# Layer 0's output projection in fixed steps on TensorE, with layer 1's first weights, K and Q beside and ahead of its last tile

## The chip, the cores and the metric

The kernel runs on one core of a Trainium2 chip. The metric is the device time of one execution in microseconds, lower is better, given as the median of three runs. A difference is read against the spread of such runs.

## The reference

A backbone of two post-norm layers over 1024 latent tokens and 256 context tokens of width 1024. Layer 0 is multi-head latent attention with 16 heads, layer 1 differential attention with 8 heads; both gate their output before the output projection. Cut to what the change touches:

```python
for i in range(DEPTH):                       # DEPTH = 2
    shift, scale, gate = adaln(c, ada_w[i], ada_b[i])
    h = x * (1.0 + scale) + shift            # the same for the context, with its own vectors
    o, o_c = mixer_i(h, h_c)                 # o is already multiplied by silu(its gate)
    x = layer_norm(ALPHA * x + gate * (o @ out_w[i]), ln_g[i], ln_b[i])
    if i < DEPTH - 1:
        ctx = layer_norm(ALPHA * ctx + gate_c * (o_c @ out_w[i]), ln_g[i], ln_b[i])

# layer 1, diff_mixer: the projections of h come first
q, k, v, gate = split(h @ w_in, 4)           # rotary on q and k, then two softmaxes a head
lam_full = exp(sum(lam[0] * lam[1])) - exp(sum(lam[2] * lam[3])) + lambda_init
```

## The kernel before

Tokens are taken in ten tiles of 128 rows: 0 to 7 are latent tokens, 8 and 9 the context. Matrix products that need the precision are made of three matmuls each, with both operands split into a high and a low part (`mm3`, lines 185 to 187; `split`, lines 176 and 177; `split16`, lines 181 and 182, which also scales).

**Layer 0's last head.** While its last step is retired, the context tiles are multiplied by their gate, turned (`turn_out`, line 833: four transposes for a half, then a split on ScalarE and VectorE, then the other half) and multiplied by the output weights (`mm_out`). This part has a written TensorE order.

**Layer 0's output.** Then comes a loop over the tiles in the order 8, 9, 0 to 7, with no written order: a planner puts the instructions of every engine, TensorE and the DMA queues too, in an order by when they can start in its own model of time. For a latent tile:

- `out_y` loads o (line 903) and its gate g (904), multiplies them on GpSimd (905), turns the product in banks "c" (833) and makes two halves y of 512 columns, in banks "a" and "b", 24 matmuls each.
- `out_z` makes z from y: times the gate row (922), plus the residual (923, loaded at 942), statistics (924, 926), 1/std on GpSimd (`rstd_of`, lines 159 and 160), and the normalisation in place (928).
- z times the norm's gain (958, VectorE) plus its bias (959, GpSimd) is written to memory for layer 1's residual (960).
- z is turned in banks "d" (965). Scale and shift, which fold the norm's gain and bias and layer 1's modulation, make h: a product on VectorE (967) and a sum on GpSimd (969), for each half. ScalarE casts h to its high part h1H (972), GpSimd makes the low part h1L (973).

The two context tiles begin at the z step, since their y is there already.

**Layer 1's start.** Behind the loop stands `prod_w(0, 0)`, the weights of Q and K of head 0: loads of two halves, squares summed on ScalarE (1026), a small matmul against ones (1029), a power-of-two scale in small steps on VectorE and GpSimd, and a split (1048). It is followed by lambda (1058 to 1072) and by a written TensorE order: K in chunks of 512, 512 and 256 tokens (`prod_k1`), Q in two chunks (`prod_q1`), with `prod_w(0, 1)`, the weights of V and the gate, woven in, then V and the gate (`prod_v1`). Attention follows in steps of one head and one tile (scores at lines 1191 and 1192); beside each step runs a part of the next head's projections, and in the last head layer 1's output.

Buffers are allotted by name from pools in order of first use, and a new pool lies over the memory of the closed one before it; a tile waits for those that lie under it.

Of the kernel before, what the change touches and what calls it, by code (L numbers as in the profile page):

```python
# [17 lines left out]
P = 128  # L18
# [35 lines left out]
def hybrid_kernel(  # L54
# [775 lines left out]
    def turn_out(o, hH_, hL_, tb, hh):  # L830

        for j in range(4):
            pe.transpose(tb[:, j * P:(j + 1) * P], o[:, (hh * 4 + j) * P:(hh * 4 + j + 1) * P], idn)
        f = lambda x: x[:, hh * 4:hh * 4 + 4, :].rearrange("p a b -> p (a b)")
        split(f(hH_), f(hL_), tb)
# [6 lines left out]
    for h in range(H0):  # L842
# [8 lines left out]
        if last:  # L851
# [16 lines left out]
            with tc.manual_schedule(engines={ENG[c] for c in MAN}):  # L868
                for t in (8, 9):
                    tb = pair()  # L870
                    for hh in range(2):
                        turn_out(octx[t][0], *tctx[t], tb[:, hh * 512:hh * 512 + 512], hh)
# [25 lines left out]
    def out_y(t, tp):  # L898

        ts = slice(t * P, (t + 1) * P)  # L900
        o = tp.tile([P, D], F32, tag="o", bufs=2, name=nm("o"))
        g = tp.tile([P, D], F32, tag="g", bufs=1, name=nm("g"))
        sp.dma_start(o, o_d[0][ts, :])
        sp.dma_start(g, sg_d[0][ts, :])
        pool.tensor_tensor(o, o, g, op=ALU.mult)
        tH = tp.tile([P, KT, P], F32R, tag="tH", bufs=2, name=nm("tH"))
        tL = tp.tile([P, KT, P], F32R, tag="tL", bufs=2, name=nm("tL"))
        for hh in range(2):
            turn_out(o, tH, tL, bank("c"), hh)
        for hh in range(2):  # L910
            y = bank("ab"[hh])
            mm_out(y, tH, tL, slice(hh * 512, hh * 512 + 512))
            yield y

    def out_z(ys, gate, res_fn, t, tp):

        z = tp.tile([P, D], F32, tag="z", bufs=2, name=nm("z"))
        res, rmul = res_fn(t)
        bs = tp.tile([P, 2, 6], F32, tag="bs", bufs=2, name=nm("bs"))
        for hh, y in enumerate(ys):  # L920
            c = slice(hh * 512, hh * 512 + 512)
            dve.tensor_tensor(z[:, c], y, gate[:, c], op=ALU.mult)
            dve.scalar_tensor_tensor(z[:, c], res[:, c], rmul, z[:, c], op0=ALU.mult, op1=ALU.add)
            dve.bn_stats(bs[:, hh, :], z[:, c])
        mv = tp.tile([P, 4], F32, tag="mv", bufs=2, name=nm("mv"))
        dve.bn_aggr(mv[:, 0:2], bs)
        rstd_of(mv[:, 2:3], mv[:, 1:2], 1.0, 1)
        dve.tensor_scalar(z, z, mv[:, 0:1], mv[:, 2:3], op0=ALU.subtract, op1=ALU.mult)
        return z

    with ow_ctx, spool("o0") as op0:
        gate = [op0.tile([P, D], F32, tag=f"gate0{s}", bufs=1, name=f"gate0{s}") for s in range(2)]
        for s in (1, 0):
            bcast_row(gate[s], gates_d[0, s:s + 1, :])
        gb = []

        zres = {}

        def res0(t):
            r = op0.tile([P, D], F32, tag="res", bufs=2, name=nm("res"))  # L940
            src = xr[t * P:(t + 1) * P, :] if t < 8 else ctxr[(t - 8) * P:(t - 7) * P, :]
            sp.dma_start(r, src)
            zres[t] = r
            return r, ALPHA

        zctx = {t: out_z([yctx[t][:, :512], yctx[t][:, 512:]], gate[1], res0, t, op0) for t in (8, 9)}
        set_banks(a=2, b=2, c=2, d=2)
        for t in (8, 9, 0, 1, 2, 3, 4, 5, 6, 7):
            if t == 0:
                for j, (src, tag) in enumerate(((ln_g, "gate01"), (ln_b, "gb1"))):  # L950
                    gb.append(op0.tile([P, D], F32, tag=tag, bufs=1, name=nm("gb")))
                    bcast_row(gb[j], src[0:1, :])
                    pool.tensor_scalar(gb[j], gb[j], ALPHA, None, op0=ALU.mult)
            s = 0 if t < 8 else 1
            z = out_z(out_y(t, op0), gate[0], res0, t, op0) if t < 8 else zctx[t]
            if t < 8:
                zr = zres[t]
                dve.tensor_tensor(zr, z, gb[0], op=ALU.mult)
                pool.tensor_tensor(zr, zr, gb[1], op=ALU.add)
                sp.dma_start(zn_d[t * P:(t + 1) * P, :], zr)  # L960
            hb = op0.tile([P, KT, P], F32, tag="hb", bufs=1, name=nm("hb"))
            for hh in range(2):
                tb = bank("d")
                for j in range(4):
                    pe.transpose(tb[:, j * P:(j + 1) * P], z[:, (hh * 4 + j) * P:(hh * 4 + j + 1) * P], idn)
                ks = slice(hh * 4, hh * 4 + 4)
                dve.tensor_tensor(hb[:, ks, :], tb.rearrange("p (a b) -> p a b", a=4),
                                  ab1[:, 0, ks, s:s + 1].to_broadcast([P, 4, P]), op=ALU.mult)
                pool.tensor_tensor(hb[:, ks, :], hb[:, ks, :],
                                   ab1[:, 1, ks, s:s + 1].to_broadcast([P, 4, P]), op=ALU.add)  # L970
            ts = slice(t * P, (t + 1) * P)
            act.copy(h1H[:, :, ts], hb)
            pool.tensor_tensor(h1L[:, :, ts], hb, h1H[:, :, ts], op=ALU.subtract)


    a1 = ctx.enter_context(ExitStack())
    wl = a1.enter_context(spool("a1"))
    TAG1 = {"p0": ([P, NTOK], F32, 2), "p1": ([P, NTOK], F32, 1), "ph": ([P, NT, P], F16, 2),
            "pl": ([P, NT, P], F16, 2), "KS0": ([P, NTOK], F16, 2), "KS1": ([P, NTOK], F16, 2),
            "QS0": ([P, SEQ], F16, 2), "QS1": ([P, SEQ], F16, 2), "Q10": ([P, SEQ], F16, 2),  # L980
            "Q11": ([P, SEQ], F16, 2), "vh": ([P, NT, P], F16, 2), "vl": ([P, NT, P], F16, 2),
            "o1": ([P, P], F32, 3), "o2": ([P, P], F32, 2), "mx": ([P, 8], F32, 2), "sm": ([P, 8], F32, 4),
            "ss": ([P, 2], F32, 2), "us": ([P, 1], F32, 3), "es": ([P, 1], F32, 3), "p2s": ([P, 2], F32, 2)}

    TAGP = {"ws": ([P, 4, 256], F32, 3), "wL": ([P, 4, 256], F16, 4), "wH": ([P, 4, 256], F16, 4),
# [9 lines left out]
    for k_, v_ in TAG1.items():  # L995
        rot(wl, v_[0], v_[1], k_, v_[2], first=True)
# [54 lines left out]
    for _ in prod_w(0, 0, lambda: bank("c"), act):  # L1051
        pass
# [476 lines left out]
```

## Time and profile before

| | us |
|---|---|
| runs shown | 1871.88, 1866.82, 1869.04 |
| median | 1869.04 |
| the profiled execution's own time | 1864.35 |
| its span, first to last instruction | 1862.5 |
| mean granted TensorE clock | 0.972 |

The span is the traced part of one execution; 1.85 us of that execution's time lie around it. Where rows of the profile are quoted, a row of a timeline gives start and length in us, engine, line, operation, output and inputs, their shapes and a count; a bracket gives the engine's idle time ahead of it and what ended it. A row of a table by stage gives its two ends and its length, the busy time and number of instructions of each engine, the granted clock, the share of the DMA engines and what they moved. A group's row has busy us, mean ns, and the idle time ahead.

### The profile page before, as it was taken

To read this page: it belongs to the slowest core of one execution; us is meant where nothing else is said; L and a number is where in the kernel's file an instruction comes from. 1 tells how busy PE (TensorE), PEld (TensorE's weight loads), DVE (VectorE), ACT (ScalarE), POOL (GpSimd) and SP (SyncE) were. 2 spreads that over 40 slices of the span, in tenths; PEclk is the share of its full clock that TensorE was granted. 3 is DMA by queue.
4 is the path that set the end of the run, shared out by engine and by line. 5 is a ranking of instruction groups with operands and counts; after the bars stand their busy time and mean duration, and the time that the engine had idled before them with its cause. 6 is when DMAs were issued, how large, how long until landed. Compare 5 with 4: busy or idle time off the path is not lost. (4 is left out here: it accounts for less than half of the span.)

```text
span 1862.5 us, 36549 instructions
## 1 busy us (share of the span) xinstructions
PE 1691.8 (91%) x14468; PEld 1235.3 (66%) x14468; DVE 1242.1 (67%) x2074; ACT 1077.1 (58%) x2143; POOL 831.5 (45%) x739
## 2 busy tenths in 40 slices
PE   7889989999999998869879899999999999988998
PEld 3888965656666565557757575767676666666776
DVE  7445765565565657435764777777877787878674
ACT  3432157877777788801123666676767676767542
POOL 1443026867767676827652313132222222423544
PEclk9999999999999999989989999999999999999999
DMA  8246630111111113134333222222211212214341
GB/s 306 64 132 181 189 107 17 39 40 30 40 44 33 44 40 101 59 130 130 122 129 104 71 62 61 60 63 62 66 52 41 50 50 50 75 42 139 100 132 68
DMA packets 111225, 154.84 MB, mean 83 GB/s; under 512 B 13415, under 2 KB 84679, under 8 KB 111054
## 3 DMA queue, kind: packets, MB, share of 16 engines
q1 hardware_dynamic: 104238, 146.22, 26.4%
q10 hardware_dynamic: 6816, 6.29, 1.0%
q8 instruction: 114, 1.87, 0.4%
q14 instruction: 57, 0.47, 0.1%
HBM read 98.65 MB, written 27.07 MB: 68 GB/s over the span
## 5 line engine op out<-in xcount | busy, mean ns | idle before, releaser
L715 POOL TENSOR_TENSOR pl<-p,ph 128x1024 f16<-128x1024 f32 (+1 forms) x176 | 364.8, 2078 | 147.4 <-ACT ph L714 119.5
L1214 ACT ACTIVATE p<-ps_b,mx 128x512 f32<-128x512 f32 (+1 forms) x384 | 230.6, 618 | 82.7 <-DVE mx L1210 82.5
L695 DVE TENSOR_REDUCE mx<-ps_a 128x1 f32<-128x1024 f32 x128 | 155.5, 1223 | 133.5 <-PE ps_a L693 133.5
L713 ACT ACTIVATE p<-ps_a,esc 128x1024 f32<-128x1024 f32 (+1 forms) x176 | 189.2, 1075 | 94.5 <-PE ps_a L771 88.0
L714 ACT CAST ph<-p 128x1024 f16<-128x1024 f32 (+1 forms) x176 | 177.1, 1006 | 5.5
L1208 DVE TENSOR_REDUCE mx<-ps_b 128x1 f32<-128x512 f32 x256 | 165.5, 681 | 0.0
L784 PE MATMUL ps_d<-Vh,pl 128*128 128x65 f16 x1344 | 145.9, 194 | 3.9 <-POOL pl L715 3.9
L781 PE MATMUL ps_d<-Vh,ph 128*128 128x65 f16 x1344 | 148.0, 195 | 0.0
L783 PE MATMUL ps_d<-Vl,ph 128*128 128x64 f16 x1344 | 146.8, 193 | 0.0
L185 PE MATMUL ps_b<-h1H,wH 128*128 128x512 f16 (+1 forms) x384 | 134.0, 349 | 13.9 <-DVE pl L182 6.8
L185 PE MATMUL ps_b<-wH,h1H 128*128 128x256 f16 x512 | 139.5, 272 | 4.7 <-ACT p L1214 4.5
L187 PE MATMUL ps_b<-wH,h1L 128*128 128x256 f16 x512 | 139.5, 273 | 0.0
L186 PE MATMUL ps_b<-wL,h1H 128*128 128x256 f16 x512 | 139.5, 273 | 0.0
L1191 PE MATMUL ps_b<-KS,QS 128*128 128x512 f16 (+1 forms) x384 | 126.5, 346 | 12.1 <-DVE pl L182 6.1
L1239 POOL TENSOR_TENSOR sm<-sm,us 128x1 f32<-128x1 f32 x64 | 16.2, 253 | 271.5 <-DVE sm L1218 267.5
L781 PEld LDWEIGHTS <-ph 128*128 128x128 f16 x1344 | 123.2, 97 | 18.3 <-issue 5.1
L187 PE MATMUL ps_b<-h1H,wL 128*128 128x512 f16 (+1 forms) x384 | 133.9, 349 | 0.8 <-DVE wL L182 0.8
L186 PE MATMUL ps_b<-h1L,wH 128*128 128x512 f16 (+1 forms) x384 | 133.9, 349 | 0.0
L783 PEld LDWEIGHTS <-ph 128*128 128x128 f16 x1344 | 123.9, 98 | 12.0
L1192 PE MATMUL ps_b<-KS,Q 128*128 128x512 f16 (+1 forms) x384 | 129.3, 345 | 0.0
L769 PE MATMUL ps_a<-qH,KH 100*128 100x512 f16 x320 | 122.0, 381 | 7.7 <-ACT p L713 3.9
L182 DVE SCALAR_TENSOR_TENSOR pl<-ps_b,lcf,ph 128x512 f16<-128x512 f32 (+1 forms) x192 | 117.4, 654 | 16.0 <-ACT ph L181 15.8
(392 smaller groups left out, 5154.7 us busy)
## 6 DMA issues: line engine op xcount, KB each, us to landing
ws<-in_dw SPq DMA_DIRECT2D x30, 512.0 KB, 3.9
adw<-in_ada_w SPq DMA_DIRECT2D x24, 512.0 KB, 4.7
adaw<-in_ada_w SPq DMA_DIRECT2D x16, 512.0 KB, 6.9
g<-sg_d SPq DMA_DIRECT2D x16, 512.0 KB, 3.8
sg_d<-gg ACTq DMA_DIRECT2D x40, 128.0 KB, 3.5
o_d<-op SPq DMA_DIRECT2D x7, 640.0 KB, 3.7
xt<-in_xT SPq DMA_DIRECT2D x16, 256.0 KB, 3.8
wgs<-in_w_in SPq DMA_DIRECT2D x32, 128.0 KB, 2.9
```

Of the source, the lines that this page charges most:

```text
L185: pe.matmul(ps, aH, bH, start=start, stop=False, skip_group_check=skip)
L186: pe.matmul(ps, aH, bL, start=False, stop=False, skip_group_check=skip)
L187: pe.matmul(ps, aL, bH, start=False, stop=stop, skip_group_check=skip)
L695: dve.tensor_reduce(mx[:, t, 0:1], ps, axis=AX.X, op=ALU.max)
L713: act.activation(p32[:, :n], st, AF.Exp, scale=esc0)
L714: act.copy(ph[:, :n], p32[:, :n])
L715: pool.tensor_tensor(pl[:, :n], p32[:, :n], ph[:, :n], op=ALU.subtract)
L781: pe.matmul(pv[:, t, :], ph[:, ts], Vh[:, k, h, :], start=(k == kcs[0] and t == 0), stop=False, skip_group_check=True)
L783: pe.matmul(pv[:, t, :V0], ph[:, ts], Vl[:, k, h, :], start=False, stop=False, skip_group_check=True)
L784: pe.matmul(pv[:, t, :], pl[:, ts], Vh[:, k, h, :], start=False, stop=(k == NT - 1), skip_group_check=True)
L1208: dve.tensor_reduce(mx[:, 2 + 2 * m + i:3 + 2 * m + i], b, axis=AX.X, op=ALU.max, negate=True)
L1214: act.activation(p[m][:, c0:c0 + n], b, AF.Exp, bias=nb, accum_out=sm[:, 2 + 3 * m + i:3 + 3 * m + i])
```

## The change

It has five parts.

1. `turn_out` makes all eight transposes, in two banks, and then both splits.
2. Layer 0's output loop is written in small steps with a fixed TensorE order. For tile t: half 0 of y(t), the turn of z(t-1), the turn of o(t+1), half 1 of y(t). Ahead of the loop stand the turn of o(0) and of z(8); z(9) is turned in tile 0. The loads of o and its gate for tiles 0 and 1 are written ahead of the context's z steps, the norm's rows later, in tile 0.
3. h's scale and shift are made by ScalarE, eight instructions of 128 columns that read the banks and take scale and shift as columns; the product on VectorE and the sum on GpSimd go.
4. Both weight preparations of head 0, `prod_w(0, 0)` and `prod_w(0, 1)`, are made in steps beside tiles 0 to 6, with their loads on ScalarE's queue, and lambda ahead of the loop.
5. Behind tile 7 and ahead of its z turn, TensorE makes K of head 0 for tokens 0 to 511; after that turn K of the context and Q for tokens 0 to 511. `prod_q1` and `prod_k1` take these as made and go on with the rest.

For this the weights of layer 1 lie in a pool of their own below layer 0's output, with high and low part in one tile; layer 1's output, at the end of the kernel, uses the same tiles again for o and its turns.

The core of the diff ("..." where lines are left out):

```diff
-    def turn_out(o, hH_, hL_, tb, hh):
-
-        for j in range(4):
-            pe.transpose(tb[:, j * P:(j + 1) * P], o[:, (hh * 4 + j) * P:(hh * 4 + j + 1) * P], idn)
-        f = lambda x: x[:, hh * 4:hh * 4 + 4, :].rearrange("p a b -> p (a b)")
-        split(f(hH_), f(hL_), tb)
+    def turn_out(o, hH_, hL_, tb):
+
+        for hh in range(2):
+            for j in range(4):
+                pe.transpose(tb[hh][:, j * P:(j + 1) * P], o[:, (hh * 4 + j) * P:(hh * 4 + j + 1) * P], idn)
+        for hh in range(2):
+            f = lambda x: x[:, hh * 4:hh * 4 + 4, :].rearrange("p a b -> p (a b)")
+            split(f(hH_), f(hL_), tb[hh])
...
-            for hh in range(2):
-                tb = bank("d")
-                for j in range(4):
-                    pe.transpose(tb[:, j * P:(j + 1) * P], z[:, (hh * 4 + j) * P:(hh * 4 + j + 1) * P], idn)
-                ks = slice(hh * 4, hh * 4 + 4)
-                dve.tensor_tensor(hb[:, ks, :], tb.rearrange("p (a b) -> p a b", a=4),
-                                  ab1[:, 0, ks, s:s + 1].to_broadcast([P, 4, P]), op=ALU.mult)
-                pool.tensor_tensor(hb[:, ks, :], hb[:, ks, :],
-                                   ab1[:, 1, ks, s:s + 1].to_broadcast([P, 4, P]), op=ALU.add)
...
-    for _ in prod_w(0, 0, lambda: bank("c"), act):
-        pass
-    set_banks(b=8)
...
+        def z_turn(t, tg="d", mid=None):
+            tb = [bank(tg), bank(tg)]
+            for hh in range(2):
+                for j in range(4):
+                    pe.transpose(tb[hh][:, j * P:(j + 1) * P], zs[t][:, (hh * 4 + j) * P:(hh * 4 + j + 1) * P], idn)
+            hb, s, ts = ot("hb", 1, [P, KT, P]), int(t > 7), rows_of(t)
+            for k in range(KT):
+                act.activation(hb[:, k, :], tb[k // 4][:, k % 4 * P:(k % 4 + 1) * P], AF.Identity,
+                               bias=ab1[:, 1, k, s:s + 1], scale=ab1[:, 0, k, s:s + 1])
+            act.copy(h1H[:, :, ts], hb)
+            pool.tensor_tensor(h1L[:, :, ts], hb, h1H[:, :, ts], op=ALU.subtract)
+
+        load_gate(1)
+        load_res(8)
+        load_o(0)
+        load_gate(0)
+        load_res(9)
+        load_o(1)
+        for t in (8, 9):
+            for hh in range(2):
+                z_half(t, hh, yctx[t][:, halves[hh]])
+            z_norm(t)
+        set_banks(a=2, b=2, c=2, d=2)
+        lambda_of()
+        pw = [prod_w(0, i, lambda: bank("c"), act) for i in range(2)]
+        wjobs = {t: [pw[i] for i in js] for t, js in enumerate(((0,), (0,), (0,), (0, 0, 1), (1,), (1,), (1, 1)))}
+        man.enter_context(tc.manual_schedule(engines={ENG["P"]}))
+        turns(0)
+        y1 = bank("b")
+        z_turn(8)
+        for t in range(8):
+            y0 = bank("a")
+            mm_out(y0, *tHL[t], halves[0])
+            z_half(t, 0, y0) if t else load_res(0)
+            for j in wjobs.get(t, ()):
+                next(j)
+            if t == 0:
+                z_half(0, 0, y0)
+                for j, (src, tag) in enumerate(((ln_g, "gate01"), (ln_b, "gb1"))):
+                    gb.append(ot(tag, 1))
+                    bcast_row(gb[j], src[0:1, :])
+                    pool.tensor_scalar(gb[j], gb[j], ALPHA, None, op0=ALU.mult)
+            z_turn(t - 1 if t else 9)
+            if t < 7:
+                turns(t + 1)
+            y1 = y1 if t == 0 else bank("b")
+            mm_out(y1, *tHL[t], halves[1])
+            z_half(t, 1, y1)
+            z_norm(t)
+            z_keep(t)
+            if t < 7:
+                load_res(t + 1)
+            if t < 6:
+                load_o(t + 2)
+        set_banks(b=8)
+        kcols, qcols = slice(P, 2 * P), slice(0, P)
+        made = {0: [*proj1(512, 0, kcols)][-1]}
+        z_turn(7, "b")
+        made[SEQ] = [*proj1(CTX, SEQ, kcols)][-1]
+        made["q"] = [*proj1(512, 0, qcols)][-1]
+        man.close()
...
-        for _ in chain(weave(chain(prod_k1(0), prod_q1(0, 0), prod_q1(0, 1)), prod_w(0, 1), WAT[0]),
+        for _ in prod_q1(0, 0, made.pop("q")):
+            pass
+        later.pop()()
+        for _ in chain(prod_k1(0, made), prod_q1(0, 1),
                        weave(prod_v1(0), prod_w(1, 0), WAT[1])):
```

The steps `load_res`, `load_o`, `turns`, `z_half` (lines 922 to 924 of before, for one half), `z_norm` (926, `rstd_of`, 928) and `z_keep` (958 to 960) hold the same instructions as `out_y` and `out_z` did.

More of the change, by code (lines that the diff above doesn't have):

```diff
@@ L915, in out_z @@
[L915 to L929, printed above, removed]
@@ L1004, in w1 @@
+    wpa = ctx.enter_context(spool("a1w"))
+    for k_, v_ in TAG1.items():
+        rot(wpa, v_[0], v_[1], k_, v_[2], first=True)
+    place = {k_: wpa for k_ in TAG1}
     def w1(tag):
@@ new lines, in hybrid_kernel @@
+    prj = ExitStack()
+    wp = prj.enter_context(spool("a1proj"))
+    for k_, v_ in TAGP.items():
+        rot(wp, v_[0], v_[1], k_, v_[2], first=True)
+    place.update({**{k_: wl for k_ in TAGL}, **{k_: wp for k_ in TAGP}})
+    TAG1.update({**TAGL, **TAGP})
+    wo4 = a1.enter_context(spool("a1ow", side="right"))
+    oHL = [[wo4.tile([P, D], F32R, name=f"oH1{k}"), wo4.tile([P, D], F32R, name=f"oL1{k}")] for k in range(NOW)]
+    gate1 = wo4.tile([P, D], F32, name="gate1")
+    cosB, sinB = w1("cosB"), w1("sinB")
```

216 lines of the change are left out of this document (101 added, 115 removed).

## The prediction

> **What bounds the kernel now.** I read the page's busy shares first, then the stretch that the change touches as a table by stage, then TensorE's timeline in it, and last the engines that TensorE waits for there.
>
> ```profile
> span 1862.5 us, 36549 instructions
> PE 1691.8 (91%) x14468; PEld 1235.3 (66%) x14468; DVE 1242.1 (67%) x2074; ACT 1077.1 (58%) x2143; POOL 831.5 (45%) x739
> ```
>
> TensorE is the bound almost everywhere, so what can be won lies where it waits or runs slow. Busy time by stage (length, then PE, PEld, DVE, ACT, POOL, granted clock, DMA share, GB/s): from the last matmul of the context rows to the end of tile 0, tiles 1 to 7, from there to layer 1's projections, and the rest of these up to the first scores.
>
> ```profile
> 822.00:854.60 32.60, 17.96 (x73) 14.19 (x73) 14.46 (x23) 3.26 (x4) 22.69 (x15) 0.74 0.47 162
> 854.60:959.50 104.90, 95.05 (x449) 75.08 (x447) 75.32 (x91) 14.45 (x21) 67.87 (x47) 0.98 0.35 119
> 959.50:974.00 14.50, 3.28 (x13) 2.32 (x14) 9.44 (x16) 6.46 (x9) 9.55 (x10) 0.64 0.57 204
> 974.00:1022.50 48.50, 48.50 (x340) 33.48 (x341) 20.61 (x49) 15.93 (x37) 11.81 (x13) 0.97 0.40 112
> ```
>
> In the first and third stretch TensorE is busy for 17.96 of 32.60 us and 3.28 of 14.50, at a clock of 0.74 and 0.64; the second is nearly full, the fourth full. ScalarE does little: 14.45 of 104.90. TensorE's timeline says which waits these are; the bracket is the idle time ahead of an instruction and who ended it:
>
> ```profile
> 791.73 0.66 PE L833 MATMUL ps_a<-idr,rsw 128*128 128x128 f32 x4 [1.40 <-DVE ows L177]
> ...
> 796.89 1.11 PE L833 MATMUL ps_a<-idr,cs 128*128 128x128 f32 x4 [1.40 <-DVE cs L177]
> ...
> 821.65 0.40 PE L187 MATMUL ps_a<-oH,cs 128*128 128x512 f32 x1
> 832.50 1.94 PE L965 MATMUL ps_d<-idr,z 128*128 128x128 f32 x8 [10.46 <-DVE z L928]
> 835.99 1.97 PE L965 MATMUL ps_d<-idr,z 128*128 128x128 f32 x8 [1.54 <-DVE hb L967]
> 840.41 1.97 PE L833 MATMUL ps_c<-idr,o 128*128 128x128 f32 x8 [2.46 <-POOL o L905]
> ...
> 854.61 1.03 PE L833 MATMUL ps_c<-idr,o 128*128 128x128 f32 x8
> ```
>
> At the head TensorE waits in turn for the normalised z of tile 8 (10.46 us), for h of tile 8 to leave its banks (1.54) and for o of tile 0 (2.46); tile 0 ends at 854.6. Inside tile 7, and behind it:
>
> ```profile
> 950.85 1.06 PE L965 MATMUL ps_d<-idr,z 128*128 128x128 f32 x8 [0.37 <-DVE z L928]
> 951.67 0.47 PE L186 MATMUL ps_a<-oL,tH 128*128 128x512 f32 x1
> 951.99 0.39 PE L187 MATMUL ps_a<-oH,tL 128*128 128x512 f32 x1
> ...
> 959.08 0.40 PE L187 MATMUL ps_b<-oH,tL 128*128 128x512 f32 x1
> 963.82 1.94 PE L965 MATMUL ps_d<-idr,z 128*128 128x128 f32 x8 [4.34 <-DVE z L928]
> 965.55 0.42 PE L1029 MATMUL ps_c<-sq,ones 128*128 128x2 f32 x2
> 972.08 0.61 PE L185 MATMUL ps_b<-h1H,wH 128*128 128x512 f16 x1 [6.11 <-ACT wH L181]
> ```
>
> Two prices come from here: 31 matmuls start between 951.99 and 959.08, so one costs 0.2287 us and half a tile (24) 5.49; eight transposes cost 0.82 (950.85 to 951.67). After the last tile TensorE waits 4.34 us for its z and 6.11 for layer 1's first weights. The chain behind a z, on VectorE, with its undisturbed and its disturbed forms:
>
> ```profile
> 830.83 1.52 DVE L928 TENSOR_SCALAR z<-z,mv 128x1024 f32<-128x1024 f32 x1 [3.20 <-POOL mv L160]
> ...
> 897.39 2.58 DVE L923 SCALAR_TENSOR_TENSOR z<-res,z 128x512 f32<-128x512 f32 x1
> ...
> 902.83 2.83 DVE L928 TENSOR_SCALAR z<-z,mv 128x1024 f32<-128x1024 f32 x1 [0.95 <-POOL mv L160]
> ...
> 959.52 0.69 DVE L922 TENSOR_TENSOR z<-ps_b,gate 128x512 f32<-128x512 f32 x1 [2.79 <-PE ps_b L187]
> 960.24 0.69 DVE L923 SCALAR_TENSOR_TENSOR z<-res,z 128x512 f32<-128x512 f32 x1
> 960.97 0.69 DVE L924 BATCH_NORM_STATS2 bs<-z 128x6 f32<-128x512 f32 x1
> 961.70 0.21 DVE L926 BATCH_NORM_AGGREGATE mv<-bs 128x2 f32<-128x12 f32 x1
> 962.86 0.81 DVE L928 TENSOR_SCALAR z<-z,mv 128x1024 f32<-128x1024 f32 x1 [0.95 <-POOL mv L160]
> ```
>
> Undisturbed, z is there 4.2 us after the tile's last matmul (959.48 to 963.67).
>
> **The change, part by part**
>
> *Context turns.* All eight transposes now run ahead of the splits, so the second four no longer wait for the first four's split. Two waits of 1.40 us go. The second turn also waits for o of tile 9, which VectorE makes beside GpSimd's work, and that stays. I take 3 us, between one wait (1.4) and both with what the next wait gives back (4).
>
> *Head, to the end of tile 0.* The new order is turns of tile 0, z of 8, half 0, z of 9, turns of tile 1, half 1: 32 transposes (3.3 us) and 48 matmuls (11.0). Ahead of it stands z of tile 8. From the tile sizes, in the order of first use, its residual lies over `rr`, which the context matmuls read to their end; so this load still starts there.
>
> ```profile
> 824.98 0.42 SPq L903 DMA_DIRECT2D o<-o_d  x1
> ```
> ```profile
> o<-o_d SPq DMA_DIRECT2D x8, 512.0 KB, 3.9
> ```
>
> The load lands 3.9 us after its issue; two L923 and two L924 (2.8), 1.16 from L926 to L928's start and 0.81 follow: 8.7, say 9.0 with the issue. The load of o of tile 0 was issued at 824.98, behind ln_g's on SP's queue; now it stands ahead of that, in free memory, and its product on GpSimd and its turn fit into the 9 us. The slow clock stays: 17.96 busy us at 0.74 against 1 are some 1.9 lost in matmuls, with the bank switches included. 9.0 + 14.3 + 1.9 = 25.2 against 32.6. I take 7 off; 2 if SP holds everything behind that residual, so that o and its gate follow it, 10 if the planner finds it another slot and the wait shrinks.
>
> *Tiles 1 to 7.* TensorE's own work is 7 x 48 x 0.2287 = 76.8, 13 turns of 0.82 = 10.7, and some 0.1 more at each return to matmuls (951.67 to 951.99 is 0.32, not 0.23): 1.3. That is 88.8 against 104.9, so 16.1 is the most that can go. Does the fixed order let it? z of the tile before is needed 5.5 us after that tile's end and is there at 4.2: covered, by 1.3. What runs on ScalarE is new: eight scale-and-shift instructions from a bank instead of two VectorE ones and two on GpSimd. Its nearest rows are a copy of the same shape from a bank, and its casts:
>
> ```profile
> L1169 ACT COPY Vf<-ps_b x80: 245/300/356, 1011.4 to 1697.0; 128x128 f32<-128x128 f32 x80
> ```
> ```profile
> L176 ACT CAST tH<-ps_c 128x512 fp32r<-128x512 f32 x14 | 7.5, 587 | 14.7 <-PE ps_c L833 14.7
> L972 ACT CAST h1H<-hb 128x1024 f16<-128x1024 f32 x7 | 7.3, 1046 | 82.4 <-POOL hb L969 82.4
> ```
>
> 8 x 0.30 + 1.05 + 2 x 0.59 = 4.6 us, starting about half-way through the z turn (0.4); the next tile wants its tH 7.1 us after half 0 ends (two turns of 0.82 and half 1). It is there at 5.0, so this too is covered, by 2.1. The Trainium skill, "ScalarE: Activation LUTs", Rules for kernel authors, speaks against such a move: additions and products belong on VectorE, and an activation costs about 0.3 us plus 0.83 ns an element. By that the eight take 3.2 us instead of 2.4 (an estimate), and 0.8 of the cover goes; the 245 to 356 ns of the copies lie under it.
>
> Against the cover stand the first weights. Their squares and splits are hidden on an idle ScalarE, but their small matmul takes one of the two banks that the turns use, and VectorE must empty it first: 1 us, twice. I add 0.5 a tile for collisions with GpSimd: 16.1 - 2 - 3.5 = 10.6. Bounds: 0 (the next part's second rival) and 14.
>
> *After tile 7.* K's first 512 columns need only tiles 0 to 3 and weights made three tiles earlier, so its 24 matmuls (5.5, by the pitch of an equally wide matmul) cover the 4.34 us for z of tile 7. Then its turn, K of the context and Q's first columns run, some 14 us in all, while h of tile 7 needs 0.8 + 4.2 more. What stays of the 14.5 us is the turn (0.8) and two matmuls (0.5): 13.2 go, and with TensorE never idle the slow clock behind it, 0.03 x 48.5 = 1.5. I take 14.7; 7.6 if the weights come late (below). The weights' four loads of 512 KB go out on ScalarE's queue, ahead of which it has nearly nothing to do, in stretches where the DMA engines are 0.35 to 0.47 busy; lambda's load and small steps lie in the 9 us for z of tile 8. I cost them at nothing; without that cover each load costs its 3.9 us once. Its memory is laid out anew, so I allow 4 us either way for what follows.
>
> Sum: 3 + 7 + 10.6 + 14.7 = 35.3. The profiled execution took 1864.35 us for a span of 1862.5; it becomes 1829.1 for 1827.2. The median of the runs shown is 1869.04, and from it I get 1834.
>
> **The rivals**
>
> *z always late (slower).* In the new order TensorE can do nothing past a z that is late. With each link in its worst form, L922 0.69, L923 2.58, L924 0.69, L926 0.2, rstd behind a GpSimd instruction (3.20), L928 2.83, z takes 10.2 us, 4.7 more than its cover. That begins to cost at 5.5 us and turns the change into a loss where each of the eight z waits costs 4.4 (35.3 / 8): z at 9.9. At 10.2 the time is 1834 + 8 x 4.7 = 1872. For it: each slow form has occurred. Against it: at 897.39 and 902.83 two of them met and the third did not, and GpSimd loses the two hb additions a tile. The skill's "GPSIMD Engine Reference", section 1, says that GpSimd shares its SBUF interfaces with VectorE and contends with instructions that have two SBUF inputs or a 2-port mode. By that rule L923 and L928 are slow whenever GpSimd runs; the trace has both forms, 0.69 and 2.58, 0.81 and 2.83, so it agrees. Chance 0.08.
>
> *The tile loop keeps its pace.* If what sets 15.0 us a tile (104.9 / 7) is VectorE's and GpSimd's collisions (75.3 and 67.9 busy of 104.9) and not the order, the 10.6 stay: 1869 - 24.7 = 1844. Chance 0.20.
>
> *The weights are not ahead.* The engines other than TensorE keep an order that is planned, not written; if the splits slip behind the last tile, the 6.11 us wait and its slow clock come back, some 7 us: 1841. The change would not do what it says. Chance 0.08.
>
> *All given back in layer 1*, by a worse order around its first scores or its output: within 0.3% of before. Chance 0.04.
>
> **How the numbers follow.** My forecast has 0.60. Its own ends are 4 + 10 + 14 + 14.7 = 42.7 us off, with up to 4 more behind (1823), and 1.4 + 2 + 6 + 13.2 = 22.6 off (1846). The 0.20 case reaches 17 off with its low ends (1.4 + 2 + 0 + 13.2). So 1823 to 1852 leaves out the slower case, the one given back and a little at the ends. A difference under 0.3% (5.6 us) can't be told from none here. Faster: 0.60 + 0.20 + 0.08 = 0.88; within: 0.04; slower: 0.08.
>
> **What would show it.** Right: the two waits of 1.40 in the context turns are gone; the first z turn waits some 9 us; tile ends 13 to 13.6 us apart; no wait of over 1 us between tile 7 and the first scores, at full clock; those come 35 us earlier. Wrong: z waits of several us in each tile, ScalarE named ahead of the turns, a wait for wH at K's start, or a time regained at 1022 that is lost again before the end.

## The result, and the profile after

The changed kernel takes 1839.58 us (median of four runs, 1836.83 to 1848.19) against 1869.79 of the kernel before on the same chip: ratio 0.9847, interval 0.9812 to 0.9883. A second series of five, below under "again", gave 1843.97 against 1870.48: 0.9862 (0.9839 to 0.9885). So it is faster by 1.4 to 1.5%, 26.5 to 30.2 us; forecast were 1834 in 1823 to 1852. The page of the first profile, an execution of 1848.19 us:

```profile
span 1846.4 us, 36569 instructions
PE 1693.7 (92%) x14468; PEld 1239.2 (67%) x14468; DVE 1240.0 (67%) x2054; ACT 1104.3 (60%) x2223; POOL 811.8 (44%) x719
```

TensorE's share of busy time rises by one point, ScalarE takes 27 us more and GpSimd 20 less. That execution began layer 0's last steps, in unchanged code, 6.7 us later than the one profiled before (store of o at 787.34 against 780.67). The other profile of the same kernel lies nearer, 2.2 us later; its stages and rows are used from here on, and called "again". The row of that store, in the timeline of before and in that of again:

```profile
780.67 1.91 SPq L797 DMA_DIRECT2D o_d<-op  x2
```
```profile
782.84 1.91 SPq L797 DMA_DIRECT2D o_d<-op  x2
```

Table by stage of again: from the last context matmul to the end of tile 0 (called the head below), tiles 1 to 7 (the loop), from there to the first scores of layer 1, and the rest.

```profile
822.50:849.00 26.50, 16.48 (x81) 13.65 (x81) 18.80 (x33) 13.48 (x29) 16.37 (x11) 0.87 0.82 283
849.00:949.85 100.85, 94.47 (x445) 76.83 (x443) 77.36 (x92) 40.57 (x85) 54.14 (x39) 0.97 0.43 141
949.85:998.10 48.25, 48.25 (x350) 34.10 (x349) 19.57 (x33) 14.37 (x35) 18.85 (x16) 1.00 0.33 92
998.10:1842.20 844.10, 773.54 (x6174) 568.85 (x6172) 633.13 (x1216) 539.96 (x1455) 277.07 (x390) 0.98 0.24 69
```

| us | before | again | difference | forecast |
|---|---|---|---|---|
| store of o to last context matmul | 41.33 | 39.66 | -1.67 | -3 |
| to the end of tile 0 | 32.6 | 26.5 | -6.1 | -7 |
| tiles 1 to 7 | 104.9 | 100.85 | -4.05 | -10.6 |
| to the first scores | 63.0 | 48.25 | -14.75 | -14.7 |
| to the end | 840.0 | 844.1 | +4.1 | 0 |

With the later start the first scores come 24.4 us earlier (1022.5 to 998.1), and the span is 20.3 shorter (1862.5 to 1842.2). What TensorE still waits for ahead of them, in its timeline of again:

```profile
797.01 1.94 PE L834 MATMUL ps_a<-idr,cs 128*128 128x128 f32 x8 [2.41 <-DVE cs L864]
...
831.12 1.97 PE L834 MATMUL ps_c<-idr,o 128*128 128x128 f32 x8 [8.50 <-POOL o L993]
...
841.61 1.06 PE L1023 MATMUL ps_d<-idr,z 128*128 128x128 f32 x8 [1.52 <-DVE z L1012]
...
870.09 1.09 PE L1023 MATMUL ps_d<-idr,z 128*128 128x128 f32 x8 [2.08 <-DVE z L1012]
...
887.18 1.10 PE L1023 MATMUL ps_d<-idr,z 128*128 128x128 f32 x8 [1.95 <-DVE z L1012]
...
930.45 1.09 PE L1023 MATMUL ps_d<-idr,z 128*128 128x128 f32 x8 [0.84 <-DVE z L1012]
```

The head's first wait is for o of tile 0, not for z of tile 8, whose turn follows it without a wait. Behind tile 7 there is none, at a clock of 1.00. In the loop tiles 1 to 7 take 13.1, 17.3, 16.7, 13.0, 14.7, 14.05 and 12.0 us: three are as short as the matmuls and turns allow. In 2, 3, 5 and 6 TensorE waits for the z of the tile before: 2.08, 1.95, 0.73 and 0.84 us. The engines behind the late z of tiles 1, 2 and 4, in order of time, from again's timeline:

```profile
865.89 2.39 POOL L993 TENSOR_TENSOR o<-o,g 128x1024 f32<-128x1024 f32 x1 [2.80 <-DMA o<-o_d]
...
868.37 0.19 POOL L159 TENSOR_SCALAR mv<-mv 128x1 f32<-128x1 f32 x1
...
869.23 0.81 DVE L1012 TENSOR_SCALAR z<-z,mv 128x1024 f32<-128x1024 f32 x1 [4.52 <-POOL mv L160]
...
878.85 3.15 DVE L182 SCALAR_TENSOR_TENSOR wx<-ws,uw,wx 128x1024 f16<-128x1024 f32 x1
...
881.92 0.68 DVE L1004 TENSOR_TENSOR z<-ps_b,gate 128x512 f32<-128x512 f32 x1
...
882.52 1.27 DVE L182 SCALAR_TENSOR_TENSOR wy<-ws,uw,wy 128x1024 f16<-128x1024 f32 x1
...
910.09 2.91 DVE L1005 SCALAR_TENSOR_TENSOR z<-res,z 128x512 f32<-128x512 f32 x1
```

In tile 1 the statistics are there at 864.7 (869.23 less 4.52), but 1/std, two small steps on GpSimd of 0.19 and 0.55 us, stands behind GpSimd's product of o. In tile 2 the two splits of layer 1's weights (wx, wy) stand around VectorE's first step on the second half of z. The first of them takes 3.15 us beside a product of o that GpSimd starts at 878.51, the second 1.27. In tile 4 no split is in the way: there a step of z takes 2.91 us instead of 0.69, beside a product of o that starts at 910.05.

### The profile page after: what moved, and what is told of

It reads as the page before. It is cut to its first block, busy times and chain, and to the rows that moved or that the text cites. A ratio compares the mean times of both kernels' runs of the same rounds, so it can differ in the third digit from the quotient of the medians.

```text
span 1846.4 us, 36569 instructions
## 1 busy us (share of the span) xinstructions
PE 1693.7 (92%) x14468; PEld 1239.2 (67%) x14468; DVE 1240.0 (67%) x2054; ACT 1104.3 (60%) x2223; POOL 811.8 (44%) x719
## 5 line engine op out<-in xcount | busy, mean ns | idle before, releaser
L784 PEld LDWEIGHTS <-pl 128*128 128x128 f16 x1344 | 123.1, 97 | 6.1 <-POOL pl L715 6.1
L181 ACT ACTIVATE ph<-ps_b,lcf 128x512 f16<-128x512 f32 (+1 forms) x192 | 115.0, 646 | 19.7 <-PE ps_b L1264 19.7
L1264 PE MATMUL ps_b<-idr,p 128*128 128x128 f32 x640 | 103.6, 278 | 24.5 <-ACT p L1251 16.3
L770 PE MATMUL ps_a<-qH,KL 96*128 96x512 f16 x320 | 122.3, 382 | 0.0
L771 PE MATMUL ps_a<-qL,KH 96*128 96x512 f16 x320 | 121.7, 380 | 0.0
L1274 PE MATMUL ps_b<-vh,pl 128*128 128x128 f16 x640 | 111.3, 220 | 5.3 <-DVE pl L182 5.3
```

What stands on the lines that cost most here:

```text
L784: pe.matmul(pv[:, t, :], pl[:, ts], Vh[:, k, h, :], start=False, stop=(k == NT - 1), skip_group_check=True)
```

## The experiments

The theory was that the loop loses to what stands ahead of z in two queues, the weights' splits on VectorE and the product of o on GpSimd, and the head to the residual of tile 8, which blocks SP. The rivals were that the start's variation makes most of it, and that VectorE and GpSimd are simply too full or in each other's way. Each kernel ran beside the kernel before on its chip; ratios are to it.

**again.** The changed kernel as it is.

> The changed kernel once more, for a second trace beside the kernels that follow. If the profiled execution of the change was an ordinary one, tiles 2 and 3 again end 15 to 16 and 18 to 19 us after the one before, tiles 1 and 4 about 13; if that was an accident of one execution, the two slow tiles stand elsewhere or are gone. The start of the stage, 6.7 us later than in the kernel before, should not come back, since no code ahead of it differs. Time 1837 to 1842 us.

Measured 1843.97 (1842.49 to 1849.86). Tiles 2 and 3 are slow again (15.8 and 19.2 us in the first profile, 17.3 and 16.7 here), so that is the kernel's. The start 6.7 us late did not come back. In the thirteen profiles of changed kernels the store lies between 780 and 789; with a single profile of the kernel before, whether one or two us of that belong to the change is open.

**w00.** K's and Q's weights of head 0 made ahead of tile 0 instead of beside tiles 0 to 3.

```diff
-  enumerate(((0,), (0,), (0,), (0, 0, 1), (1,), (1,), (1, 1)))
+  enumerate(((), (), (), (1,), (1,), (1,), (1, 1)))
...
   y1 = bank("b")
+  for _ in pw[0]: pass
   z_turn(8)
```

> Layer 1's weights of head 0 for K and Q are made in the wait at the head, ahead of the first z turn, instead of in tiles 0 to 3; those for V stay in tiles 3 to 6. If the weights' preparation is what the tile loop lost (my theory): tile 3 falls from 19.2 to about 13 us and tile 2 from 15.9 to about 15, since 1.91 us of that tile is the wait for a normalised z whose 1/sqrt stood behind the 2.4 us product of o on GpSimd; 6 to 7 us less in all, 1833. If GpSimd's and VectorE's collisions in general set the pace: another tile takes over the loss, within 2 us of the changed kernel. If the preparation delays z of tiles 8 and 9 at the head instead: the head grows by 1 to 3 us and the gain is 3 to 5.

Measured 1848.88, 0.9889 (0.9867 to 0.9911). Stages of w00, head and loop, and then a row of TensorE's timeline:

```profile
825.40:859.50 34.10, 18.34 (x83) 15.38 (x83) 21.93 (x41) 16.80 (x34) 17.38 (x12) 0.70 0.76 266
859.50:954.50 95.00, 91.20 (x443) 73.93 (x441) 71.57 (x84) 37.27 (x82) 53.50 (x37) 1.00 0.41 133
```
```profile
843.15 0.59 PE L927 MATMUL ps_c<-sq,ones 128*128 128x2 f32 x2 [7.20 <-ACT wsq L924]
```

The loop is shorter by 5.85 and tile 3 back at 13.1. Tile 3 is the clear part: it takes 16.5 to 19.5 us in the eight profiles that have these weights beside tiles 0 to 3, and 13.0 to 13.9 in the five that have not. The run moves the whole preparation, so it does not tell the splits from the small matmul and the scale steps. Nor is the 5.85 a clean price: 0.97 against 1.00 of the granted clock is in it, and resd below, with the weights in their old place, has a loop of 97.2. In total the kernel got slower, where 1833 was expected. The time is lost at the head, where the weights' small matmul stands ahead of the z turn and waits 7.2 us for its squares, whose buffer lambda's load uses too. That is this arrangement's fault.

**wout.** V's and the gate's weights out of the loop as well, behind tile 7's turn.

```diff
+  enumerate(((), (), (), (), (1,), (1,)))      # loads and squares only
...
   z_turn(7, "b")
+  for _ in pw[1]: pass
```

> As the kernel before it in this list, and the weights for V are also taken out of the loop: their loads and squares lie in tiles 4 and 5, the small matmul and the splits behind the last tile's turn. No split is left in the tile loop. By my theory tiles 5 and 6 fall from 13.8 and 14.0 to 13.0 (another 1.5 to 2 us), 1831; the loop is then 7 x 13 + 2 for the GpSimd wait of tile 2 = 92 to 94 us. If collisions in general set the pace: the loop stays at 98 or more. Should the splits now delay the first K columns' successors, a wait appears between the last tile and the first scores, and the gain is given back.

Measured 1846.35, 0.9877 (0.9853 to 0.9901). The head is as long as in w00. Tiles 5 and 6 go from 13.7 and 14.0 in w00 to 13.1 and 13.0, so what left them cost 1.6 us together, but the loop stays at 95.35: in tile 1, 17.5 us long, 1/std now stands behind GpSimd's product and h1L. Its row in TensorE's timeline of wout:

```profile
863.26 1.67 PE L1023 MATMUL ps_d<-idr,z 128*128 128x128 f32 x8 [2.62 <-DVE z L1012]
```

**res.** Only the order of first use in the new pool: `gate01`, `hb` and `gb1` first, so that tile 8's residual no longer lies over `rr`.

```diff
+  held = {tag: [ot(tag, 1, sh)] for tag, sh in
+          (("gate01", [P, D]), ("hb", [P, KT, P]), ("gb1", [P, D]))}
```

> Only the order in which the tiles get their memory differs: the first residual, o and z no longer lie over what the context matmuls read, so their loads can start at about 817 instead of 827 us. By my theory the 8.6 us wait for the first turn is the late load (3.9), two additions and statistics (2.6), and a product of o behind it: it goes, the head falls from 25.9 to 16 to 18 us, and the time by 8 to 10, 1830. If the wait is set by something else, a queue behind the last store of o or GpSimd's product: the head falls by 0 to 3 us.

Measured 1841.24, 0.9839 (0.9816 to 0.9863), which in total can't be told from the changed kernel's 0.9847 and 0.9862; the head takes 23.6 instead of 26.5, where 16 to 18 were expected. The turn of o waits 0.86 us instead of 8.50. Now z of tile 8 is late, in the timeline of res:

```profile
823.48 0.69 DVE L1005 TENSOR_TENSOR z<-ps_a,gate 128x512 f32<-128x512 f32 x1 [4.35 <-PE ps_a L187]
...
831.13 1.97 PE L1024 MATMUL ps_d<-idr,z 128*128 128x128 f32 x8 [5.74 <-DVE z L1013]
```

VectorE had tile 9's first step, which needs the last context matmul, ahead of what was left of tile 8's z.

**resd.** res, with VectorE held to the written order for the z of tiles 8 and 9.

```diff
-  for t in (8, 9): ...
+  with tc.manual_schedule(engines={ENG["D"]}):
+      for t in (8, 9): ...
```

> The kernel with the moved memory, and VectorE's instructions for the context rows' z in the order of the program, so that tile 8's no longer stand behind the first product of tile 9, which waits for the last context matmul. In the run before, that order kept the first z turn 5.74 us back though every load had landed. By my theory z of tile 8 is then ready before the context matmuls end, the 5.74 us go, the head is 16 to 18 us (23.7 there), and the time 5 to 7 us less. If the wait is made by something else on the way to z, the head stays at 22 or more.

Measured 1838.3, 0.9842 (0.9819 to 0.9865), no more than res; the head takes 24.7, not 16 to 18. TensorE in the timeline of resd:

```profile
824.25 1.09 PE L1024 MATMUL ps_d<-idr,z 128*128 128x128 f32 x8 [0.68 <-DVE z L1013]
...
831.14 0.80 PE L187 MATMUL ps_a<-oH,tL 128*128 128x512 f32 x1 [5.33 <-DVE tL L177]
```

The z turn's wait is gone and stands, nearly as long, at tile 0's matmuls, whose split now follows tile 9's z on VectorE. A wait taken away at one place came back at the next.

**pg.** GpSimd in written order inside the loop, with the product of o directly behind 1/std.

```diff
-  man.enter_context(tc.manual_schedule(engines={ENG["P"]}))
+  man.enter_context(tc.manual_schedule(engines={ENG["P"], ENG["G"]}))
...  # next after z_half(t, 0, y0):
+      if t < 6: load_o(t + 2)
+      if t: z_keep(t - 1)
```

> GpSimd keeps the order of the program inside the tile loop, the product of o for two tiles ahead is written before the 1/sqrt of z, and the stored z of a tile one tile later. No 1/sqrt can then stand behind a product of o. By my theory the waits for z in tiles 2 and 6 (about 2 and 0.8 us) go and the one in tile 3 stays, because that one is VectorE's weight split: loop 97 to 99 us instead of 100.9, 2 to 4 us less in all. If GpSimd's order is not it: no change in those waits.

Measured 1845.09, 0.988 (0.9858 to 0.9902): no gain, loop 102.5 instead of the expected 97 to 99. The timeline of pg shows what took its place:

```profile
858.16 2.35 POOL L993 TENSOR_TENSOR o<-o,g 128x1024 f32<-128x1024 f32 x1
...
858.23 2.83 DVE L1012 TENSOR_SCALAR z<-z,mv 128x1024 f32<-128x1024 f32 x1 [2.53 <-POOL mv L160]
```

The product starts 0.07 us ahead of the last step of z, which takes 2.83 us beside it instead of 0.81.

**zz.** For the 4.1 us lost later: the last output weights of layer 1 through two buffers, not four.

```diff
-  z = [w1("z"), w1("res")][k % 2]
+  z = w1("z")
```

> Only the end of layer 1 differs: the last four output weights go through two buffers instead of four, so that two of the four scalings on VectorE come behind the join of the last head's second tile and not ahead of it, as in the kernel before the change. The changed kernel gains 24.4 us up to layer 1's first scores and keeps 20.3: 4.4 us are lost between the last head's second and fourth step. If the loss is the four scalings ahead of that join: 2 to 4 us come back. If it is the earlier products of o on GpSimd that slow VectorE down: under 1 us comes back.

Measured 1837.62, 0.9833 (0.9806 to 0.9859); first scores to end 837.7 instead of 844.1. VectorE around the last join of p, from the timelines of before, again and zz:

```profile
1720.39 2.84 DVE L1220 SCALAR_TENSOR_TENSOR p<-p,sm,p 128x1280 f32<-128x1280 f32 x1
...
1723.15 1.27 DVE L1276 SCALAR_TENSOR_TENSOR res<-res,gsub,gate 128x1024 f32<-128x1024 f32 x1
```
```profile
1692.29 3.36 DVE L1313 SCALAR_TENSOR_TENSOR z<-z,gsub,gate 128x1024 f32<-128x1024 f32 x1
...
1696.31 2.65 DVE L1313 SCALAR_TENSOR_TENSOR res<-res,gsub,gate 128x1024 f32<-128x1024 f32 x1
...
1701.29 3.67 DVE L1257 SCALAR_TENSOR_TENSOR p<-p,sm,p 128x1280 f32<-128x1280 f32 x1
```
```profile
1696.66 3.69 DVE L1257 SCALAR_TENSOR_TENSOR p<-p,sm,p 128x1280 f32<-128x1280 f32 x1
...
1700.29 1.28 DVE L1313 SCALAR_TENSOR_TENSOR z<-z,gsub,gate 128x1024 f32<-128x1024 f32 x1
```

In the changed kernel all four scalings of the last weights run ahead of the join, 2.4 to 3.4 us each; before, one did. With two buffers half of them can't start so early, and the loss is gone. The total alone (0.9833) is not clear of the changed kernel's, but the stage is: 842.9 to 846.3 us in the nine profiles with four buffers, 837.7 to 839.9 in the four with two. Why the scalings came so early is less well shown. The last of their loads is issued 2.0 us ahead of the start of the join before this one (1681.25 against 1683.24), and before the change it came 1.4 us behind it; that buffers freed earlier allow it is my reading.

**all2.** res, resd, pg, wout's placing and zz in one kernel, as first put together.

> All of it together: the moved memory, VectorE's order at the head, GpSimd's order in the loop, head 0's weights made at the head (squares ahead of lambda's small steps, which use the same buffer) or behind the last turn, and two buffers for the last output weights. If the terms add up, head 17 and loop 92 to 93 instead of 26.5 and 100.9, and 2 to 4 at the end: 18 to 22 us less than the changed kernel, about 1822. If the weights' steps take back what the head gains, 1828 to 1832.

Measured 1842.76, 0.9862 (0.984 to 0.9884). Head 24.9 and loop 96.5, with pg's slow last step of z (2.87 us) ahead of the turns in tiles 1 to 5; 55.5 to the first scores, with V's weights late. The parts don't add up (1822 was expected if they did), since each moves work into another's cover.

**u_sc.** Part 3 of the change undone: scale and shift of h on VectorE and GpSimd again.

```diff
-  for k in range(KT):
-      act.activation(hb[:, k, :], tb[k // 4][...], AF.Identity, bias=ab1[...], scale=ab1[...])
+  for hh in range(2):
+      dve.tensor_tensor(hb[:, ks, :], tb[hh]..., ab1[:, 0, ...], op=ALU.mult)
+      pool.tensor_tensor(hb[:, ks, :], hb[:, ks, :], ab1[:, 1, ...], op=ALU.add)
```

> The changed kernel, but h's scale and shift again by VectorE (two products of 128x512 a tile) and GpSimd (two additions), as before the change; all else is the change's. If what the loop gained rests on the move to ScalarE (GpSimd loses 8 of its 64 to 68 us and stands less in the way of z): the waits for z grow in most tiles and the loop goes from 100.9 back to 104 us or more, 1846 to 1852. If it rests on the order alone: the loop stays within 2 us, 1842 to 1846.

Measured 1853.06, 0.9915 (0.9886 to 0.9944). The loop's row in the table by stage of u_sc, and tile 1 in its timeline:

```profile
847.90:961.95 114.05, 98.44 (x445) 80.62 (x443) 82.63 (x107) 22.98 (x30) 76.22 (x57) 0.93 0.38 124
```
```profile
848.68 2.49 POOL L1029 TENSOR_TENSOR hb<-hb,ab 128x512 f32<-128x512 f32 x2
...
852.32 2.14 POOL L1032 TENSOR_TENSOR h1L<-hb,h1H 128x1024 f16<-128x1024 f32 x1 [1.16 <-ACT h1H L1031]
...
854.42 2.34 POOL L993 TENSOR_TENSOR o<-o,g 128x1024 f32<-128x1024 f32 x1
...
856.84 0.19 POOL L159 TENSOR_SCALAR mv<-mv 128x1 f32<-128x1 f32 x1
...
857.72 0.81 DVE L1012 TENSOR_SCALAR z<-z,mv 128x1024 f32<-128x1024 f32 x1 [6.48 <-POOL mv L160]
...
858.67 1.94 PE L1023 MATMUL ps_d<-idr,z 128*128 128x128 f32 x8 [5.02 <-DVE z L1012]
```

The loop is 13.2 us longer than in the full change and 9.15 longer than before. With the order fixed and the additions back on GpSimd (76.2 busy us in the loop, 54.1 in again), 1/std stands behind the product and behind h1L, which comes after the additions, and TensorE waits 5.02 us in tile 1 (4.66 and 3.05 in two others). The comparison with the kernel before is not one of the order alone, since here the weights are made in the loop, too.

**u_kq.** Part 5 undone in one place: tile 7's z turn ahead of K.

```diff
+  z_turn(7, "b")
   made = {0: [*proj1(512, 0, kcols)][-1]}
-  z_turn(7, "b")
```

> The changed kernel, but the turn of the last tile's z stands ahead of layer 1's first K columns, so nothing covers the way from the last matmul to z. By my theory the wait of 4.2 us that the kernel before had there comes back, and some of the slow clock behind it (up to 1.5): from the last tile's end to the first scores 52.5 to 54 instead of 48.3 us, 1848 to 1850. If weights that are ready are the greater part and z was no wait of its own: under 2 us.

Measured 1848.42, 0.9898 (0.9872 to 0.9924); 54.5 to the first scores instead of 48.25. The wait of before (4.34) is back, in TensorE's timeline of u_kq:

```profile
952.46 1.16 PE L1023 MATMUL ps_b<-idr,z 128*128 128x128 f32 x8 [4.33 <-DVE z L1012]
```

**all7.** The parts together, rearranged: zz; res; VectorE's and TensorE's order written for the z of 8, the turn of o(0) and the z of 9; GpSimd's order in the loop with the keeping of z ahead of the product of o; the norm's rows scaled by ScalarE; both weights out of tiles 1 to 6 but for V's loads and squares; lambda's small steps in tile 2.

```diff
+  z_half(8, ...); z_norm(8); turn_out(ol[0], ...); z_half(9, ...); z_norm(9)
...  # next after z_half(t, 0, y0):
+      if t: z_keep(t - 1)
+      if t < 6: load_o(t + 2)
...
-  pool.tensor_scalar(gb[j], gb[j], ALPHA, None, op0=ALU.mult)
+  act.activation(gb[j], gb[j], AF.Copy, scale=ALPHA)
```

> The causes that the runs so far named, each answered: the moved memory; at the head z of tile 8, the turns of tile 0 and its splits, then z of tile 9, in that order on VectorE; ln_g and ln_b scaled by ScalarE; the weights of head 0 for K at the head and for V behind the last turn, lambda's small steps in tile 2; GpSimd in the order of the program, with a product of o behind the addition to the stored z and not right behind the 1/sqrt, where it made the last step of z take 2.8 instead of 0.8 us; two buffers for the last output weights. By my theory the head falls from 26.5 to about 17, the loop from 100.9 to 92 to 94, the end keeps its 6.6: 1820 to 1826. If a new wait takes the place of each that goes, as in the two combinations before: 1832 or more.

Measured 1829.03 (1826.25 to 1831.08), 0.979 (0.9765 to 0.9815): the best version, below both kernels, though above the 1820 to 1826 that were expected. Stages of all7, then its timeline:

```profile
820.85:844.25 23.40, 17.21 (x84) 14.49 (x84) 17.87 (x29) 13.74 (x28) 11.65 (x11) 0.85 0.77 267
844.25:934.00 89.75, 89.75 (x441) 74.08 (x440) 64.24 (x85) 36.28 (x83) 52.05 (x34) 1.00 0.37 133
934.00:987.40 53.40, 50.44 (x352) 35.20 (x351) 24.45 (x41) 17.40 (x39) 18.75 (x19) 0.97 0.36 103
```
```profile
828.20 0.56 PE L927 MATMUL ps_c<-sq,ones 128*128 128x2 f32 x2 [4.61 <-DVE z L1005]
...
949.00 3.17 DVE L1318 SCALAR_TENSOR_TENSOR gate<-ws,sc,gate 128x1024 f32<-128x1024 f32 x1 [4.48 <-DMA ws<-in_ada_w]
...
972.25 0.47 PE L1222 MATMUL ps_b<-idr,rr 128*128 128x128 f32 x1 [2.64 <-ACT rr L1212]
```

TensorE is busy in all 89.75 us of the loop: what again loses there, 11.1 us, goes away by order and placing. GpSimd does nearly the same work in the loop (52.05 busy us against 54.14), so it was not too full. For VectorE that is not shown, since 13 us of its work have left the loop (64.24 against 77.36). The last step of z takes 0.81 us in every tile here, so the collisions that are left lie where nothing waits. The head keeps 4.61 us, since the weights' small matmul takes a bank that still holds tile 9's sums. Behind tile 7, 5.15 us are given back: V's late weights hold the load buffers, the load for the gate row of layer 1 is issued at 944.21 (927.08 in again), VectorE waits 4.48 us for it with layer 1's first Q and K behind it, and at the end of that chain a turn waits 2.64.

**all9.** all7 with the small matmul moved into tile 0, V's weights back into tiles 4 to 6, and the memory laid out once more, so that the gate, the residuals, o and the norm's rows can load under the context matmuls.

```diff
+  wjobs: ((0, 0, 0), (), (), (), (1,), (1,), (1, 1, 1))
```

> As the last combination, with its two remaining losses answered. First, its head still took 23.3 us: the small matmul of the weights, ahead of the z turn, sat in a bank over tile 9's context sums and waited 4.6 us for VectorE to read them; here it follows half 0 of tile 0 in a free bank, and the memory is laid out once more, so that gate, residuals, o and ln_b are loaded under the context matmuls. Second, V's weights behind the last turn held their load buffers and so delayed what layer 1 loads next, and 53.4 us passed from the last tile to the first scores, not 48.3; here they are made in tile 6. By my theory head 16 to 18 us, loop 90 to 92, then 48 to 50: 9 to 12 us less than that combination, 1817 to 1821. If the head's wait is only handed on again (to z of tile 9 or the splits of tile 0): head 20 or more, and 1823 to 1827.

Measured 1832.83, 0.9801 (0.9776 to 0.9826), no better than all7, where 1817 to 1821 was expected. The head falls to 20.25, but the loop is 93.15 again and the stretch to the first scores 56.85. The timelines of TensorE, SP and VectorE of all9:

```profile
979.49 0.48 PE L1219 MATMUL ps_b<-idr,rr 128*128 128x128 f32 x1 [5.91 <-ACT rr L1209]
```
```profile
955.08 0.33 SPq L1018 DMA_DIRECT2D zn_d<-res  x1
955.47 0.43 SPq L1127 DMA_DIRECT2D cosB<-in_cs  x1
```
```profile
960.31 0.69 DVE L1144 TENSOR_TENSOR rr<-ps_b,cosB 128x512 f32<-128x512 f32 x1 [7.43 <-DMA cosB<-in_cs]
```

The gate row is early again (943.31 instead of 949.00 in all7), but another load took its place: the rotary table `cosB` is issued 0.39 us behind the store of tile 7's z, which waits for GpSimd, at 955.47 instead of 946.35 in again, and VectorE waits 7.43 us for it.

## Why the prediction was right and wrong

Direction, range and the stretch behind tile 7 were right. The head came out nearly right by a route that the text had not taken, which is luck, and three terms were off. Of the 35.3 us of the sum 26.5 to 30.2 were measured, and the time lies 5.6 and 10.0 us above the forecast in the two series.

- *After tile 7*, 14.7 forecast, 14.75 measured, by its own steps: K covers z, the weights are there, the clock is 1.00. u_kq takes the cover away and 6.25 us come back: 4.33 of waiting, and slow clock behind it (0.54 over the next 3.4 us).
- *Context turns*, 3 forecast, 1.7 measured (1.4 on the mean of the changed kernels). The two waits of 1.40 are gone, but half of that is given back ahead of the turns. In again the second turn waits 2.41 us for o of tile 9: that wait, which the text says "stays", grew from 1.74. In nine other profiles of changed kernels it is the first turn that waits, 2.89 us instead of 0.83, and the second waits 1.31 to 1.89.
- *Head*, 7 forecast, 6.1 measured, right in size by another route. The step that failed is "now it stands ahead of that, in free memory". The timeline of again has the residual of tile 8 ahead of o on SP, held up to the last context matmul, and o is issued 0.38 us behind it, its gate another 0.52 later:

```profile
822.46 0.33 SPq L987 DMA_DIRECT2D res<-in_ctxr  x1
822.84 0.42 SPq L991 DMA_DIRECT2D o<-o_d  x1
```

  I had priced this case at 2 instead of 7 off. It cost no more because o and the residual load side by side: the turn of o waits 8.50 us, and z of tile 8 is there behind it. In the sum's own terms the wait was 8.50 instead of 9.0, with 1.52 for z of tile 9 on top, and TensorE's busy time 16.48 instead of 16.2; how the 1.9 of slow clock in that was got can't be followed from the rows. The case named for 10 off, another slot for the residual, was res: 9.0 off (32.6 to 23.6), with the wait moved to z.
- *Tiles 1 to 7*, 10.6 forecast, 4.05 measured: the mis-sized term. The floor was nearly right (88.8 forecast; all7 89.75). Over that floor I allowed 2 us for the weights and 3.5 for collisions; again has 11.1. TensorE's waits make 6.4 of it: 5.6 for the four late z and 0.8 for the bank of the weights' small matmul, which I had priced at 2. The rest is the slower clock (0.97 against 1.00) and the small matmuls. I had counted the bank, but not that each split, up to 3.15 us, stands in VectorE's queue in front of z, nor that 1/std can stand behind a product on GpSimd; and a collision can cost z 2.2 us in one tile (2.91 against 0.69), where I had 0.5.
- *What carries the loop's gain* was wrong, too. The sum gave it all to the fixed order, and took ScalarE's eight instructions as a cost to be covered. u_sc shows that without them the loop is 13.2 us longer, and loses 9.15 us against before; how much of the 9.15 the order makes and how much the weights in the loop is open, as the order alone was not run. The rival "z always late" was real, at most 5 us a wait; that GpSimd loses two additions a tile stood there only as a point against it, and is what keeps it small. With 4.05 of 10.6 us won, the loop also lies nearer to the second rival, "The tile loop keeps its pace", which gave 1844. Its reason holds in part: the late z of tile 4 and the long form of the split in tile 2 are collisions with GpSimd. But they don't set the pace, since in all7 none of them binds. The third rival, "The weights are not ahead", did not happen, since TensorE waits nowhere for a weight behind tile 7.
- *What follows*, 0 forecast with 4 either way: 4.1 lost, just past the 4 allowed and found by zz in layer 1's output. The sign of being wrong, a time regained at the first scores and lost again before the end, is there in that size.

ScalarE's eight took 2.90 us, between the 2.4 of the copies' row and 3.2. Row of again's timeline:

```profile
855.45 2.90 ACT L1026 ACTIVATE hb<-ps_d,ab 128x128 f32<-128x128 f32 x8 [8.30 <-PE ps_d L1023]
```

The 3.2 was the estimate by the Trainium skill, "ScalarE: Activation LUTs", Rules for kernel authors; it was the nearer one. The Trainium skill's advice there, VectorE and not ScalarE for additions and products, did not pay here: u_sc put the work back on VectorE and GpSimd, and the loop grew by 13.2 us, with ScalarE busy for 23.0 of its 114.05 us and GpSimd in the path of z. VectorE alone was not run. The Trainium skill's "GPSIMD Engine Reference", section 1, names the contention of GpSimd with VectorE; the rows of pg (2.83 against 0.81) and of again and zz (3.36 against 1.28) agree.

A wait can cost more than its length: behind 5.02 us in u_sc the turn itself takes 1.94 us instead of 1.09, and behind 5.33 in resd a matmul 0.80 instead of 0.40. The granted clock says how: taken over these rows it is 0.50, against 1.00 over the turns of 1.09 and 1.10 in again. The length of the wait alone does not tell when. The context turn of again runs at 0.50 behind 2.41 us, and the turn behind 4.33 us in u_kq takes 1.16 at 0.86, with 0.54 over the 3.4 us that follow. What decides it is open.

## What to carry to other kernels

Before an order is fixed on one engine, go through the queues of the engines that make its late operands, and count what a planner may put ahead of the small steps there: here the 0.7 us of 1/std stood behind 2.4 us of product, and a step of z behind 3.15 us of weights. Relieve the engine in that path, too: the same order without that relief (u_sc) was 9.15 us slower in the loop than no fixed order. A wait that is taken away at one engine shows up at the next in line, so orders are changed together and then read again, also far behind the change, wherever its memory is used a second time.

## What the runs showed of the hardware

- The last step of z (128x1024) takes 0.81 us alone and 2.83 to 2.87 when a GpSimd product starts 0.07 us before it; the product itself takes 2.34 to 2.40. That is not so everywhere: beside the scalings of the last weights in again three GpSimd subtractions of 128x1024 in a row take 3.33 to 3.34 us, and the next one 2.34.
- A scale and shift of 128x128 from a bank on ScalarE is 468 ns in the mean, and eight in a row take 2.90 us, less than eight times that, so they overlap. Their row in the groups by line of the first profile of the changed kernel:

```profile
L1026 ACT ACTIVATE hb<-ps_d,ab 128x128 f32<-128x128 f32 x72 | 26.1, 468 | 46.2 <-PE ps_d L1023 46.2
```

- TensorE's granted clock was 0.50 over a turn of 1.94 us (u_sc) and 1.00 over one of 1.09 (again), with the same eight transposes.
- The same unchanged code reached the store of o between 780 and 789 us in the fourteen profiles, a spread as large as the smaller terms of this sum.
